# A two-layer decoder trunk on one core: seven block products in the first feed-forward, stacked attention values, state-space tables prepared earlier and read two blocks ahead

## The chip, the core and the metric

The kernel runs on one core of a Trainium2 chip. The core has TensorE (PE in the rows: matrix products, with PEld for its weight loads), VectorE (DVE), ScalarE (ACT), GpSimd (POOL) and the DMA queues, which are fed by SyncE (SP). The metric is the device time of one launch in microseconds (us). Before the change the median of three runs is 2345.22 us (2342.04 to 2348.31).

## The reference

The input is one sequence of 1024 positions with 1024 channels, in float32. There are two layers, each of a mixer and a gated convolutional feed-forward; all add to the residual `x`:

```python
for layer in range(DEPTH):
    i = layer // 2
    if layer % 2 == 0:
        x = x + mla_shortconv_mixer(rms_norm(x, attn_norm[i]), ...)
    else:
        x = x + s5_mixer(rms_norm(x, ssm_norm[i]), ...)
    x = x + conv_ffn(rms_norm(x, ffn_norm[layer]), ...)

def conv_ffn(h, w_up, conv_w, w_down):
    up = causal_depthwise_conv(h @ w_up, conv_w)      # 1024 -> 2 x 2816, width 3
    gate, val = jnp.split(up, 2, axis=-1)
    return (jax.nn.silu(gate) * val) @ w_down
```

The first mixer is causal attention (8 heads, 64 value channels each) beside a short gated convolution. The second is a state-space layer: 64 groups of 16 channels share a complex state of 64. Its coefficients (`exp`, `sin`, `cos` of the inputs `lambda`, `log_step`, and products with `b` and `c`) don't depend on `x`; from them come tables that the layer multiplies with.

## The kernel before

Channels lie on partitions and positions along the rows; the residual stays on the chip as eight tiles `xT0` to `xT7` of 128 x 1024. Each float32 operand of a product is split into a high and a low part (ACT copies the high part, DVE or POOL subtracts), and three of the four part products are summed (`PASSES`). A 128 x 512 product is one `MATMUL`; each has its own weight load.

The stages, in the order of the span: the short convolution with its products (0 to 198 us), attention (to 511.6), the first feed-forward (to 1294), the state-space layer with its gated linear unit (to 1640), the second feed-forward (to the end).

**Short convolution.** `first_units` computes the first three of twelve units (48 matmuls each, line 175) while the norm's sums are still computed; then each of four blocks `m` has three units (`c`, `i`, `b`), which DVE scales (268) and convolves (282 to 290). Two `down` products (190) follow, whose results DVE adds to the residual (193).

**Attention.** Written out by hand under `tc.manual_schedule()`. The values' products (634) take 64 columns of the values' high part or low part as weights, with 128 positions of the probabilities moving, three per block of keys. ACT copies the result (655), splits its high part (657) and POOL its low part (658).

**First feed-forward, `ffn(0, ...)`, 747 on.** The last attention rows go through the output product (`down(last_at, ...)`), with the norm's sums beside it (`Boundary`). Then 44 units of 48 matmuls; DVE scales and convolves each (759 to 764) and multiplies gate and value (808). After each two blocks `down` adds two rows of the second product: eleven groups, 16 evictions each (193). In the gaps `background()` issues one step of `Params` (845 on), which builds the state-space tables: `base` (some 195 small DVE operations on 128 x 32, lines 868 to 891), 16 units (a complex product 1042 to 1047, outer products 1055 to 1060, PE transposes and small products), and 16 `turns` (1055 to 1060 too). The tables go to DRAM.

**State-space layer.** A list `order` fixes the program under `tc.manual_schedule()`. `load_states(m)` and `load_outputs(m)` read the tables of block `m` one block ahead: `et`, `tt` and `co` have one buffer each.

**Second feed-forward.** Class `Pair` (1601 on): gate and value columns of a block and the two halves of positions form a 2 x 2 block product, which takes seven products of 12 matmuls (1648) instead of eight. Sums of weights (1614) and of inputs (`NormBoundary.second_half`, 1504) come first; the gated values go to DRAM (`gfd`) and are read again for the second product in groups of four rows, split again by ACT, DVE and POOL (1794 to 1796).

Outside the sections by hand, a scheduler in the compiler puts each engine's instructions in an order by when they should be ready; each engine then works through its own queue strictly in that order.

## Time and profile before

| | |
|---|---|
| median of the runs | 2345.22 us |
| profiled execution | 2344.66 us, of which the span is 2342.9 |
| PE busy | 2248.5 us (96%) |
| DVE busy | 1614.7 us (69%) |
| ACT, POOL busy | 851.3 us, 767.0 us |
| matmuls on PE | 11228 recorded |

The time of a run is the span of the profile and 1.8 us around it. PE's busy time includes the modelled end of a pipelined matmul, so a stage is read better by its matmuls and by how far apart they start. In the table of stages each engine has its busy time and its instructions in brackets; the granted clock of TensorE is given as a share of 2.4 GHz.

### The profile page before, as it was taken

To read this page: it belongs to the slowest core of one execution; us is meant where nothing else is said; L and a number is where in the kernel's file an instruction comes from. 1 tells how busy PE (TensorE), PEld (TensorE's weight loads), DVE (VectorE), ACT (ScalarE), POOL (GpSimd) and SP (SyncE) were. 2 spreads that over 40 slices of the span, in tenths; PEclk is the share of its full clock that TensorE was granted. 3 is DMA by queue.
4 is the path that set the end of the run, shared out by engine and by line. 5 is a ranking of instruction groups with operands and counts; after the bars stand their busy time and mean duration, and the time that the engine had idled before them with its cause. 6 is when DMAs were issued, how large, how long until landed. Compare 5 with 4: busy or idle time off the path is not lost.

```text
span 2342.9 us, 29810 instructions
## 1 busy us (share of the span) xinstructions
PE 2248.5 (96%) x11228; PEld 1867.9 (80%) x11228; DVE 1614.7 (69%) x2650; ACT 851.3 (36%) x1446; POOL 767.0 (33%) x575
## 2 busy tenths in 40 slices
PE   7999899999999999999999988999789999999999
PEld 6888888888788878888888877788568888878887
DVE  6344677787978778879777487323888888876542
ACT  4112566664232333332223255312444444443110
POOL 4322454435233222232224344431043333324220
PEclk9999999999999999999999998999999999999999
DMA  4112000012122221223332288521132222245301
GB/s 155 45 38 57 1 10 10 10 46 72 29 66 62 82 68 49 76 80 92 101 102 63 93 223 242 171 72 41 54 110 93 82 81 81 81 153 181 125 10 72
DMA packets 227152, 192.04 MB, mean 82 GB/s; under 512 B 25472, under 2 KB 202944, under 8 KB 227008
## 3 DMA queue, kind: packets, MB, share of 16 engines
q1 hardware_dynamic: 227008, 190.14, 26.9%
q8 instruction: 88, 1.44, 0.2%
q14 instruction: 56, 0.46, 0.1%
HBM read 148.22 MB, written 46.07 MB: 83 GB/s over the span
## 4 chain that ended last, share of the span: by engine, by line
PE 79%; DVE 11%; issue 3%; DMA 3%; ACT 3%; POOL 1%; SPq 0%; DVEq 0%; POOLq 0%; ACTq 0%
PE pu L175 31%; PE pd L190 22%; PE pc L1648 4%; PE pb L1648 4%; PE pa L1648 4%; PE pd L1648 2%; PE pu L1554 1%; PE pss L586 1%; PE po L634 1%; PE pckv L378 1%; PE pq L446 1%; PE ptp L615 1%; DVE xT L1696 1%; PE pcq L378 1%; PE pda L644 1%
## 5 line engine op out<-in xcount | busy, mean ns | idle before, releaser
L154 POOL TENSOR_TENSOR wl<-raw,wh 128x1024 fp32r<-128x1024 f32 (+2 forms) x115 | 289.1, 2515 | 487.3 <-ACT wh L153 242.3
L193 DVE TENSOR_TENSOR xT<-pd,xT 128x512 f32<-128x512 f32 x320 | 204.3, 682 | 160.4 <-PE pd L190 159.8
L153 ACT ACTIVATE wh<-raw 128x1024 fp32r<-128x1024 f32 (+2 forms) x117 | 122.4, 1051 | 305.8 <-PE pu L175 212.6
L175 PE MATMUL pu<-f_h,wh 128*128 128x512 f32 x704 | 219.4, 393 | 0.0
L175 PE MATMUL pu<-f_l,wh 128*128 128x512 f32 x704 | 217.2, 390 | 0.0
L175 PE MATMUL pu<-f_h,wl 128*128 128x512 f32 x704 | 216.7, 389 | 0.0
L175 PEld LDWEIGHTS pu<-f_l,wh 128*128 128x128 f32 x704 | 132.1, 188 | 27.9
L175 PEld LDWEIGHTS pu<-f_h,wl 128*128 128x128 f32 x704 | 132.1, 188 | 27.9
L175 PEld LDWEIGHTS pu<-f_h,wh 128*128 128x128 f32 x704 | 130.7, 188 | 28.7 <-issue 1.7
L810 POOL TENSOR_TENSOR gl<-c,gh 128x512 fp32r<-128x512 f32 x44 | 61.4, 1415 | 247.0 <-ACT gh L809 247.0
L1696 DVE SCALAR_TENSOR_TENSOR xT<-u,vec,xT 128x1024 f32<-128x1024 f32 x84 | 111.1, 1330 | 13.3 <-ACT xT L1694 12.6
L759 DVE TENSOR_TENSOR u<-pu,f_rb 128x512 f32<-128x512 f32 x88 | 56.8, 685 | 89.9 <-PE pu L175 87.9
L190 PE MATMUL pd<-gh,wh 128*128 128x512 f32 x352 | 113.5, 403 | 5.4 <-DVE u L759 2.9
L190 PE MATMUL pd<-gh,dwh 128*128 128x512 f32 x352 | 108.8, 390 | 2.5 <-DVE xT L193 1.5
L190 PE MATMUL pd<-gl,wh 128*128 128x512 f32 x352 | 110.4, 395 | 0.0
L190 PE MATMUL pd<-gh,wl 128*128 128x512 f32 x352 | 110.0, 394 | 0.0
L190 PE MATMUL pd<-gh,dwl 128*128 128x512 f32 x352 | 108.5, 389 | 0.0
L190 PE MATMUL pd<-gl,dwh 128*128 128x512 f32 x352 | 108.4, 389 | 0.0
L1796 POOL TENSOR_TENSOR dwl<-raw,dwh 128x1024 fp32r<-128x1024 f32 x20 | 60.8, 3066 | 112.5 <-PE pd L190 84.3
L761 ACT ACTIVATE c<-u,vec 128x512 f32<-128x512 f32 x88 | 59.9, 717 | 69.5 <-DVE u L759 69.1
L190 PEld LDWEIGHTS pd<-gh,wh 128*128 128x128 f32 x352 | 65.8, 191 | 22.6 <-DVE xT L193 4.0
L190 PEld LDWEIGHTS pd<-gh,dwh 128*128 128x128 f32 x352 | 66.1, 188 | 16.9 <-DVE xT L193 1.9
(569 smaller groups left out, 5790.6 us busy)
## 6 DMA issues: line engine op xcount, KB each, us to landing
raw<-in_ffn_w_up_dram SPq DMA_DIRECT2D x50, 512.0 KB, 3.8
raw<-in_ffn_w_down_dram SPq DMA_DIRECT2D x42, 512.0 KB, 4.4
xT<-in_ffn_w_up_dram SPq DMA_DIRECT2D x40, 512.0 KB, 3.6
gfd<-xT SPq DMA_DIRECT2D x21, 512.0 KB, 2.6
raw<-gfd SPq DMA_DIRECT2D x20, 512.0 KB, 4.0
raw<-in_w_glu_dram SPq DMA_DIRECT2D x16, 512.0 KB, 4.0
raw<-in_mix_w_in_dram SPq DMA_DIRECT2D x14, 512.0 KB, 3.9
xT<-in_xt_dram SPq DMA_DIRECT2D x8, 512.0 KB, 7.6
```

Of the source, the lines that this page charges most:

```text
L153: nc.scalar.activation(h[:, 0:n], raw[:, 0:n], AF.Copy)
L154: eng.tensor_tensor(out=l[:, 0:n], in0=raw[:, 0:n], in1=h[:, 0:n].bitcast(F32), op=ALU.subtract)
L175: nc.tensor.matmul(ps[hf], lhsT=w[wi][:, P * k:P * k + P], rhs=xs[k][xi][:, HALVES[hf]], start=(k == 0 and wi == 0 and xi == 0), stop=(k = ...
L190: nc.tensor.matmul(ps[hf], lhsT=ws[i][wi][:, P * f:P * f + P], rhs=gts[i][xi][:, HALVES[hf]], start=(i == first and wi == 0 and xi == 0), ...
L193: nc.vector.tensor_tensor(out=xT[f][:, HALVES[hf]], in0=ps[hf], in1=xT[f][:, HALVES[hf]], op=ALU.add)
L378: nc.tensor.matmul(ps[:, HALF * j:HALF * j + n], lhsT=xa[k][xi][:, P * (2 * p + j):P * (2 * p + j) + P], rhs=w[k // kw][wi][:, n * (k % kw ...
L759: nc.vector.tensor_tensor(out=u[:, 2:HALF + 2], in0=ps[hf], in1=rb[:, HALVES[hf]], op=ALU.mult)
L761: nc.scalar.activation(c, u[:, 2:HALF + 2], AF.Copy, scale=cwcol(layer, 2, m))
L810: nc.gpsimd.tensor_tensor(out=gl[:, cols], in0=cv[hf], in1=gh[:, cols].bitcast(F32), op=ALU.subtract)
L1648: nc.tensor.matmul(ps, lhsT=w[:, HALF * wi + P * k:HALF * wi + P * k + P], rhs=x.at(xi, k), start=(start and k == 0 and wi == 0 and xi == ...
L1696: nc.vector.scalar_tensor_tensor(out=c, in0=u[:, w:S + w], scalar=cwcol(self.layer, w, m), in1=c, op0=ALU.mult, op1=ALU.add)
L1796: eng.tensor_tensor(out=l, in0=raw, in1=h.bitcast(F32), op=ALU.subtract)
```

## The change

Four parts, and in the text that follows they keep their numbers.

1. The first feed-forward uses the code of the second (`FeedForward`, and `Pair` with it): 44 x 42 = 1848 matmuls in the up-product where there were 44 x 48 = 2112. The output product before it is done one half of the positions after the other (16 banks of 512), so that the first half's norm (`sums`, `spread`, `first_half`) can begin before the second is done. The weights of the first blocks are no longer read and split within attention. Gated values go through DRAM, and so does the residual; the second product runs in groups of 2, 4, 4, 4, 4, 2 and 2 rows (112 evictions where there were 176).
2. Values in attention: the high and low parts of the values stand beside each other in one stationary block of 128 columns; two products per block of keys (576 in all) take the place of three (864). The halves of the result are added at the end: ACT copies the lower 64 partitions, DVE adds the upper ones (32 additions of 64 x 256).
3. `Params` in two parts. `base` and units 0 to 7 run in the short convolution: six steps in each of four blocks `m`, the rest in the two `down` products. What they keep goes to DRAM (`kpd`) and comes back. Units 8 to 15 and the turns run in the first feed-forward's second product, one step after each `f`.
4. State-space layer: `et` and `co` get two buffers; the first tables are read during the first units, and then two blocks ahead (`tt` one).

```diff
+        def units(self, first, end):
+            self.end = end
+            self.loaded = self.load(first)
+            for q in range(first, end):
+                yield from self.unit(q)
...
+        def first_part(self):
+
+            yield from self.base()
+            for j in range(2):
+                V.tensor_copy(out=self.apow[j][:, :, 1], in_=self.a[1][j])
+            self.powers(self.apow, ((1, 1, 2, self.a[1]), (1, 2, 3, self.a[2]), (1, 4, 5, self.a[4])))
+            yield
+            yield from self.units(0, SPLIT)
+            nc.sync.dma_start(out=kpd, in_=self.keep)
+            yield
+
+        def second_part(self):
+
+            nc.sync.dma_start(out=self.keep, in_=kpd)
+            yield from self.units(SPLIT, NP // 2)
...
+            yield
+            for q in range(NP // 2):
+                if q % 2 == 0:
+                    j = q // 2
+                    src = kd[:, GC * j:GC * j + P].rearrange("(g c) n -> c g n", c=GC)
+                    nc.sync.dma_start(out=ttd[GC * j:GC * j + GC], in_=src)
+                yield from self.turns(q)
+            yield
+
+    params = Params()
...
+    params.open("a")
+    stages = params.run(params.first_part())
+
+    def background(n=1):
+        for _ in range(n):
+            next(stages, None)
+
...
             ui = scaled(ps_i, "ui")
+            background(2)
...
             held_down = (gts, wr)
         else:
-            down(*held_down)
-            down(gts, wr)
+            down(*held_down, after=lambda f: background(f % 2))
+            down(gts, wr, after=lambda f: background(f % 2))
...
-                    vv = vt.rearrange("p (t i h n) -> p t i h n", t=2, i=4, h=2)
-                    self.vh, self.vl = vv[:, 0], vv[:, 1]
+                    vv = vt.rearrange("p (i h t n) -> p i h t n", t=2, i=4, h=2)
+                    self.vh, self.vl = vv[:, :, :, 0], vv[:, :, :, 1]
+                    self.v = vt.rearrange("p (i h n) -> p i h n", i=4, h=2)
...
             def values(self, po, c0):
                 for kb in range(self.qb + 1):
                     sk = self.steps[kb // 4]
-                    for vi, pi in PASSES:
-                        nc.tensor.matmul(po[0:VD, c0:c0 + P], lhsT=(sk.vh, sk.vl)[vi][:, kb % 4, self.h, :],
+
+                    for pi in range(2):
+                        nc.tensor.matmul(po[:, c0:c0 + P], lhsT=sk.v[:, kb % 4, self.h, :],
                                          rhs=self.pt[kb // 4][pi][:, P * (kb % 4):P * (kb % 4) + P],
-                                         start=(kb == 0 and vi == 0 and pi == 0), stop=(kb == self.qb and vi == 1))
+                                         start=(kb == 0 and pi == 0), stop=(kb == self.qb and pi == 1))
 
...
         def finish_pair(grp, po, hf, i2):
             a32 = small([P, 256], "a32", "a32", 1)
             for h in range(2):
-                nc.scalar.activation(a32[VD * h:VD * h + VD, :], po[0:VD, 256 * h:256 * h + 256], AF.Copy)
+                rows, both = slice(VD * h, VD * h + VD), slice(256 * h, 256 * h + 256)
+                nc.scalar.activation(a32[rows, :], po[VD:P, both], AF.Copy)
...
-            up_first = [split_w(r) for r in up_raw]
...
+    last_rows, last_w = [groups[gr].at for gr in (2, 3)], [w_rows[gr] for gr in (2, 3)]
+    ff = FeedForward(0)
+    for hf in range(2):
+        for f in range(KT):
+            ps = psum("pd")
+            first = 1 if f < 3 else 0
+            for i in range(first, 2):
+                for wi, xi in PASSES:
+                    nc.tensor.matmul(ps, lhsT=last_w[i][wi][:, P * f:P * f + P], rhs=last_rows[i][xi][:, HALVES[hf]],
+                                     start=(i == first and wi == 0 and xi == 0), stop=(i == 1 and wi == 1))
+            if hf and f == 2:
+                ff.sums(0)
+            x = xT[f][:, HALVES[hf]]
+            nc.vector.tensor_tensor(out=x, in0=ps, in1=x, op=ALU.add)
+            ff.add(f, hf)
+            if hf and f == 5:
+                ff.spread(0)
+                ff.first_half()
     if "x1" in dbg:
...
-    down(last_at, w_last, after=bd, skip=3)
...
+    ff.up()
+    groups_d = [(0, 2)] + [(r, r + 4) for r in range(2, 18, 4)] + [(18, 20), (20, 22)]
+    ready_d = ff.begin_down(groups_d[0])
+    params.open("b")
+    stages = params.run(params.second_part())
+    for n in range(len(groups_d) - 1):
+        gts, ws = ready_d
+        last = n == len(groups_d) - 2
+        ready_d = ff.rows(*groups_d[n + 1], ff.d_tile if last else atile)
+        down(gts, ws, after=lambda f: background())
+    for _ in stages:
+        pass
...
-            et, cs = tab("et")[:, 0], tab("cs", 2, 2)
+            et, cs = tab("et", 1, 2)[:, 0], tab("cs", 2, 2)
...
+        def load_tt(m):
+            tables["t", m] = tab("tt")[:, 0]
+            nc.sync.dma_start(out=tables["t", m], in_=ttd[:, 8 * m:8 * m + 8, :])
+
+        def load_co(m):
+            tables["c", m] = tab("co", 1, 2)[:, 0]
+            nc.sync.dma_start(out=tables["c", m], in_=cpd.rearrange("r s g n -> (r s) g n")[:, 8 * m:8 * m + 8, :])
...
-        ps, rb = first_units([split_w(loads.pop(0)()) for m in range(3)], bd.xs, bd, rbp)
+        first_w = [split_w(loads.pop(0)()) for m in range(3)]
+        p5 = p5s.enter_context(phase("ps5"))
+        load_states(0)
+        load_tt(0)
+        load_co(0)
+        raw = [loads.pop(0)()]
+        load_states(1)
+        load_co(1)
+        ps, rb = first_units(first_w, bd.xs, bd, rbp)
...
             states(m)
-            if m + 1 < KT:
-                load_states(m + 1)
+            if m + 2 < KT:
+                load_states(m + 2)
 
         def step_outputs(m):
             emit(m)
             if m + 1 < KT:
-                load_outputs(m + 1)
+                load_tt(m + 1)
+            if m + 2 < KT:
+                load_co(m + 2)
```

The rest of the diff moves `Params`, `Blocks`, the norm's class and `Pair` up in the file and gives them the layer as an argument.

In the order that the compiler gives, the first place is TensorE in the short convolution, block `m` = 1, after its second unit. Before (`a0_h`, `a0_l` are the normed input, `wh`, `wl` the weights):

```order
L175 MATMUL pu_447<-a0_h7_171,wl_444 128x512
L175 MATMUL pu_448<-a0_h7_171,wl_444 128x512
L175 MATMUL pu_511<-a0_h0_124,wh_507 128x512 [waits DVE_49]
L175 MATMUL pu_512<-a0_h0_124,wh_507 128x512 [waits DVE_49]
L175 MATMUL pu_511<-a0_l0_125,wh_507 128x512
L175 MATMUL pu_512<-a0_l0_125,wh_507 128x512
```

And now (`pct`, `pet` and `pk` are the banks of a table's unit; `z0`, `z1` its outer products, `ct` its input):

```order
L175 MATMUL pu_690<-a0_h7_178,wl_687 128x512
L175 MATMUL pu_691<-a0_h7_178,wl_687 128x512
L518 MATMUL pct_788<-ident_72,ct_781 128x64 [waits DMAHW2_49,DMAHW1_49,DVE_49]
L544 MATMUL pet_840<-ident_72,z0_784 128x2x64 [waits DVE_49]
L555 MATMUL pk_849<-z0_784,bd0_804 32x128 [waits DVE_49,Activation_49]
L175 MATMUL pu_861<-a0_h0_131,wh_857 128x512
...
L175 MATMUL pu_861<-a0_l2_144,wh_857 128x512
L544 MATMUL pet_840<-ident_72,z1_785 128x2x64 [waits DVE_49]
L544 MATMUL pet_840<-ident_72,z0_784 128x2x64
L544 MATMUL pet_840<-ident_72,z1_785 128x2x64
```

The third unit of the block now stands behind a transpose and two small products of table unit 0, which wait for DVE.

VectorE in the same stretch; before, from the first block's scaling on (`uc`, `ui`, `ub` are the scaled units, `ut` and `cv` the convolution's):

```order
L268 TENSOR_TENSOR uc_359<-pu_178,a0_rb_324 128x512 [waits Activation_49]
L268 TENSOR_TENSOR uc_359<-pu_179,a0_rb_324 128x512 [waits Activation_49]
L268 TENSOR_TENSOR ui_362<-pu_180,a0_rb_324 128x512
L268 TENSOR_TENSOR ui_362<-pu_181,a0_rb_324 128x512
L282 TENSOR_TENSOR ut_365<-uc_359,ui_362 128x1024 [waits DVE_49]
L285 SCALAR_TENSOR_TENSOR cv_368<-ut_365,vec_84,cv_368 128x1024 [waits Activation_49,Pool_49]
L268 TENSOR_TENSOR ub_372<-pu_298,a0_rb_324 128x512 [waits PE_49]
L287 SCALAR_TENSOR_TENSOR cv_368<-ut_365,vec_84,cv_368 128x1024 [waits DVE_49]
```

And now, the stretch in which `z0` is finished (`keepa` holds the coefficients, `scr` scratch, `om0` a part of the outer product):

```order
L689 TENSOR_TENSOR ut_810<-uc_683,ui_740 128x1024
L304 TENSOR_TENSOR keepa_366<-keepa_366,scr_380 128x32 [waits DVE_49]
L304 TENSOR_TENSOR keepa_366<-keepa_366,scr_380 128x32
L490 TENSOR_TENSOR om1_825<-sr0_786,keepa_366 128x256
L304 TENSOR_TENSOR scr_380<-keepa_366 128x32 [waits DVE_49]
L304 TENSOR_TENSOR scr_380<-keepa_366 128x32
L317 SCALAR_TENSOR_TENSOR keepa_366<-keepa_366 128x32
L491 TENSOR_TENSOR z0_784<-z0_784,om0_824 128x2x128
L304 TENSOR_TENSOR keepa_366<-scr_380 128x32 [waits DVE_49]
L304 TENSOR_TENSOR scr_380<-keepa_366 128x32 [waits DVE_49]
L692 SCALAR_TENSOR_TENSOR cv_813<-ut_810,vec_84,cv_813 128x1024 [waits Activation_49]
L304 TENSOR_TENSOR scr_380<-keepa_366 128x32 [waits DVE_49]
```

Small steps of `base` (128 x 32) and outer products stand between the convolution's operations, each of which waited only for its own input before.

TensorE in attention, a retired item's values; before:

```order
L634 MATMUL po_2220<-ph_2234,vt_1709 64x128 [waits Activation_49]
L634 MATMUL po_2220<-pl_2235,vt_1709 64x128
L634 MATMUL po_2220<-ph_2234,vt_1709 64x128 x2
L634 MATMUL po_2220<-pl_2235,vt_1709 64x128
L634 MATMUL po_2220<-ph_2234,vt_1709 64x128
...
L634 MATMUL po_2220<-pair_2275,vt_1709 64x128 [waits Activation_49]
L634 MATMUL po_2220<-pair_2275,vt_1709 64x128 x5
```

And now, at the same place:

```order
L1048 MATMUL po_3084<-ph_3097,vt_2573 128x128 [waits Activation_49]
L1048 MATMUL po_3084<-pl_3098,vt_2573 128x128
L1048 MATMUL po_3084<-ph_3097,vt_2573 128x128
L1048 MATMUL po_3084<-pl_3098,vt_2573 128x128
...
L1048 MATMUL po_3084<-pair_3137,vt_2573 128x128 [waits Activation_49]
L1048 MATMUL po_3084<-pair_3137,vt_2573 128x128 x3
```

Six and six products with 64 columns of weights (an `x` and a number count equal rows) have become four and four with 128: the output has 128 partitions of `po` now and had 64.

TensorE at the entry of the first feed-forward, which did not exist in this form (`pd` the output product, `f0_st1` the second half's sums, `b11` the first input block, `w1` the split weights of a block):

```order
L1518 MATMUL pd_6528<-ath3_5808,wh_6088 128x512
L1518 MATMUL pd_6528<-atl3_5809,wh_6088 128x512
L1518 MATMUL pd_6528<-ath3_5808,wl_6089 128x512
L1225 MATMUL f0_st1_6609<-ones_77,f0_sq1_6317 128x2 [waits DVE_49]
L1225 MATMUL f0_st1_6609<-ones_77,f0_sq1_6317 128x2 x2
L1451 MATMUL pa_6570<-b11h0_6322,w1_6548 128x512 [waits Activation_49]
L1451 MATMUL pa_6570<-b11l0_6324,w1_6548 128x512
L1451 MATMUL pa_6570<-b11h0_6322,w1_6548 128x512 [waits DVE_49]
L1451 MATMUL pa_6570<-b11h0_6322,w1_6548 128x512
L1451 MATMUL pa_6570<-b11l0_6324,w1_6548 128x512
```

The first block product stands behind the output product and the sums, and waits for ACT's and DVE's splits of input and weights.

## Rows read from the trace of the kernel before

**Rows 1.** Page, part 1: busy us, share of the span, instructions.
```profile
PE 2248.5 (96%) x11228; PEld 1867.9 (80%) x11228; DVE 1614.7 (69%) x2650; ACT 851.3 (36%) x1446; POOL 767.0 (33%) x575
```

**Rows 2.** Stages: length, then each engine's busy us (instructions), clock, DMA share, GB/s.
```profile
1760.00:2095.00 335.00, 333.85 (x1473) 276.11 (x1473) 281.29 (x294) 149.45 (x204) 104.52 (x100) 1.00 0.27 90
```

**Rows 3.** PE's waits, 1640 to 1770 us: total us, times, longest.
```profile
PE pa L1648 <- ACT w L1637: 4.0, 1, 4.0
```

**Rows 4.** Stages, entry of the second feed-forward.
```profile
1640.00:1661.00 21.00, 15.72 (x63) 12.18 (x63) 11.93 (x24) 8.45 (x15) 1.47 (x3) 0.92 0.22 62
1661.00:1760.00 99.00, 83.92 (x324) 62.45 (x323) 89.76 (x122) 46.60 (x70) 27.97 (x20) 0.95 0.28 88
```

**Rows 5.** Stages, entry and body of the first feed-forward.
```profile
623.00:651.00 28.00, 22.84 (x85) 17.43 (x83) 27.69 (x118) 4.65 (x10) 2.99 (x2) 0.88 0.08 20
651.00:1249.00 598.00, 597.74 (x2718) 484.28 (x2717) 470.65 (x897) 181.51 (x367) 182.43 (x89) 1.00 0.28 78
```

**Rows 6.** Groups of DVE, 511.6 to 1294 us: busy, mean ns, idle before.
```profile
L1055 DVE TENSOR_TENSOR z<-sr,ap 128x256 f32<-128x256 f32 (+1 forms) x32 | 18.8, 588 | 0.0
...
L1057 DVE TENSOR_TENSOR z<-sr,ap 128x256 f32<-128x256 f32 (+1 forms) x32 | 15.8, 494 | 1.2 <-DMA cpd<-z 1.1
...
L1045 DVE TENSOR_TENSOR cm<-bt,zi 128x32 f32<-128x32 f32 x16 | 9.6, 597 | 27.0 <-DMA bt<-in_b_re_dram 27.0
...
L1047 DVE TENSOR_TENSOR sr<-cm,cm 128x32 f32<-128x32 f32 x16 | 2.9, 180 | 0.0
```

**Rows 7.** DVE of line 868 alone, 511.6 to 1294 us: length, busy (instructions).
```profile
511.60:1294.00 782.40, 21.56 (x105) 1.00 0.26 71
```

**Rows 8.** Groups of DVE, second feed-forward's second product.
```profile
L193 DVE TENSOR_TENSOR xT<-pd,xT 128x512 f32<-128x512 f32 x95 | 60.8, 684 | 117.2 <-PE pd L190 117.2
L1796 DVE TENSOR_TENSOR gl<-raw,gh 128x1024 fp32r<-128x1024 f32 x20 | 49.7, 2514 | 6.6 <-ACT gh L1795 6.6
```

**Rows 9.** Stages, short convolution after its first units.
```profile
52.80:152.80 100.00, 100.00 (x443) 82.78 (x442) 41.09 (x34) 17.64 (x17) 30.82 (x15) 1.00 0.17 48
152.80:198.00 45.20, 44.95 (x193) 35.79 (x191) 24.02 (x34) 4.77 (x5) 10.24 (x5) 1.00 0.12 33
```

**Rows 10.** PE's timeline, scores in attention: start us, length.
```profile
455.20 0.27 PE L586 MATMUL pss<-kh,qh 96*128 96x128 f32 x1
...
455.54 0.28 PE L590 MATMUL pss<-tri,eye 128*128 128x128 f32 x1
```

**Rows 11.** PE's timeline, values in attention.
```profile
459.22 0.28 PE L634 MATMUL po<-ph,vt 128*64 128x128 f32 x2
459.34 0.22 PE L634 MATMUL po<-pl,vt 128*64 128x128 f32 x1
459.40 0.28 PE L634 MATMUL po<-ph,vt 128*64 128x128 f32 x2
```

**Rows 12.** Groups of PE's weight loads in attention, shapes apart: busy, mean ns.
```profile
L634 PEld LDWEIGHTS po<-pair,vt 128*64 128x64 f32 x432 | 30.2, 135 | 0.4
...
L586 PEld LDWEIGHTS pss<-kl,qh 96*128 96x128 f32 x96 | 18.5, 193 | 1.4
```

**Rows 13.** Stages, attention from 260 us.
```profile
260.00:511.60 251.60, 231.59 (x2007) 211.12 (x2004) 195.90 (x390) 156.39 (x376) 105.26 (x178) 0.99 0.05 16
```

**Rows 14.** Stages, state-space layer to 1500 us.
```profile
1294.00:1400.00 106.00, 100.18 (x510) 84.16 (x509) 61.29 (x91) 41.60 (x53) 45.67 (x25) 0.97 0.58 160
1400.00:1500.00 100.00, 81.35 (x439) 69.90 (x438) 62.90 (x93) 51.95 (x69) 38.66 (x23) 0.90 0.77 223
```

**Rows 15.** PE's waits, 1294 to 1500 us.
```profile
PE px L1288 <- DMA gd<-gy: 9.4, 1, 9.4
```

More of the change, by code (lines that the diff above doesn't have):

```diff
@@ L1708, in hybrid_trunk_kernel @@
-    pairs = [Pair(1, m) for m in range(FIRST + 1)]
-    early = pairs[0:FIRST]
-    for p in pairs:
-        p.weights("12")
-    pps.close()
-    pbk = pps.enter_context(tc.tile_pool(name="psu", bufs=1, space=PSUM, reuse_waits="tile"))
-    def bank_tile(bank, name):
-        return pbk.tile([P, HALF], F32, tag=f"ps{bank}", bufs={"a": 3, "b": 2, "c": 2, "d": 1}[bank], name=name)
-    xb = {"1": nb.b11, "2": nb.b21}
-    for p in pairs:
-        p.product("1", "a", True)
-    nb.sums(1)
-    pbt.close()
@@ L1723, in hybrid_trunk_kernel @@
-    puc = ctx.enter_context(ExitStack())
-    pU = puc.enter_context(phase("pu"))
-    for p in pairs:
-        p.keep()
-    for p in early:
-        p.sums()
-        p.weights("56")
-    blocks = nb.second_half()
-    pairs[0].product("2", "a", False)
-    nb.spread(1)
-    xb["5"] = next(blocks)
-    for p in pairs[1:]:
-        p.product("2", "a", False)
-    xb["6"] = next(blocks)
-    for p in early:
-        p.weights("74")
-    pairs[0].evict()
-    for j in "56":
-        for p in early:
-            p.run(j)
@@ L1743, in hybrid_trunk_kernel @@
-    for p in early:
-        p.weights("3")
-    for j in "74":
-        xb[j] = next(blocks)
-        early[0].run(j)
-        early[1].product(j, "b" if j == "7" else "d", j == "4")
-        if j == "7":
-            early[1].add(early[1].p1, "b", early[1].p1)
-    pairs[FIRST].load(False)
-    pairs[FIRST].sums()
-    pairs[FIRST].weights("65743")
-    xb["3"] = next(blocks)
-    early[0].run("3")
-    early[0].finish()
-    for j in "65":
-        pairs[FIRST].run(j)
-    early[1].evict()
-    early[1].lower("c", HALF)
```

1346 lines of the change are left out of this document (650 added, 696 removed).

## Prediction

> **What bounds the kernel now.** I read the page's busy shares first, then the table of stages, then in each stage that the change touches the waits or groups that price it. The busy shares name the engine: PE is busy for 96% of the span, DVE for 69% [rows 1]. So a removed matmul is a gain of its own length wherever PE runs without a break, and a new wait of PE is a loss of its own length. One stage gives the price of a matmul: from 1760 to 2095 us PE has no gap to speak of and starts 1473 matmuls in 335 us, 0.2274 us each [rows 2]. DVE's mean share hides where it is short: at the entry of the second feed-forward it is busy for 89.8 of 99 us while PE gets only 324 matmuls, 73.7 us' worth [rows 4]; in the short convolution it is busy for 41.1 of 100 and 24.0 of 45.2 us [rows 9]; in the first feed-forward for 470.7 of 598, with PE never short [rows 5]. The change takes matmuls from PE and moves DVE's work about. So the question is where DVE's work lands, and whether PE's queue stands behind it.
>
> **1, the up-product.** 2112 − 1848 = 264 matmuls less, at 0.2274 us: −60.0 us, all on the path, since PE had no gap from 651 us on [rows 5].
>
> **1, the entry.** The same code's entry is to be seen in the second feed-forward: from 1640 to 1760 us it took 120 us for 63 + 324 = 387 matmuls, 88.0 us' worth, so 32 us were lost to waits and to the lower clock behind them (0.92 and 0.95) [rows 4]; the first product waited 4.0 us for a split weight [rows 3]. In the first feed-forward there is less to hide behind. The output product is 78 matmuls, 17.7 us. The first half's sums come after 48 of them, at some 11 us. Then DVE has eight norm multiplications, eight splits and six weight splits of 128 x 512, three evictions and the small chain of the norm. I price the 25 large ones like an eviction of that size, 0.68 us [rows 8], 17 us, and the chain at 3: it ends some 31 us after the start, against 17.7 when PE is done. That is 13 us of waiting where the second feed-forward had 4.0, so 9 more, and I take 12 with the clock that falls in a break of that length. The old entry goes: 5.2 us of gap and 0.12 of 28 us of clock [rows 5], with a little before it some 10 us. Net 32 + 12 − 10 = **+34 us**. Bounds: +15, if the splits hide behind PE as in the second feed-forward and the whole queue is shorter by the weights that are ready; +50, if the second half's norm is late by as much again.
>
> **1 and 3, the second product.** Eviction count falls from 176 to 112; this is DVE's time, not PE's. But DVE gets the splits of the gated values that come back, 2.51 us each [rows 8], and the steps of `Params`. One unit costs DVE (102.9 + 30.8)/16 = 8.4 us: six groups of outer products between 18.8 and 15.8 us, 102.9 together, and six of the complex product between 9.6 and 2.9, 30.8 together [rows 6]. The first group of two rows is 96 matmuls, 21.8 us of PE, and carries eight steps (2.7 units, 22 us), 16 evictions (11 us) and four splits (10 us): 43 us of DVE. The next two groups, 43.7 us of PE each, carry the same 43. So DVE has 129 us of work in 109 us. Evictions lag by the banks that there are, and the ends of DVE's operations overlap by some tenth in the sums of groups, which leaves 116. I take **+8 us**, near what is left of 116 − 109; bounds 0 (the surplus runs off in the lighter groups behind) and +25. A table unit's small products on PE move from one full stage of PE to another: nothing.
>
> **3, the short convolution.** PE had no gap from 52.8 to 198 us, and DVE had 41.1 + 24.0 = 65.1 us of work in these 145.2 us [rows 9]. Added: `base`, some 195 operations at 21.56/105 = 0.205 us [rows 7], 40 us, and eight units at 8.4 us, 67 us. Total 172 us, or 160 with the overlapped ends taken off the added part. Even packed without a gap it is 15 to 27 us more than the stage has. And it isn't packed, since PE stands in line with it. In the new order PE meets the first table unit's three instructions behind block 1's second unit, which at PE's price is near 77 us. They wait for `z0`, behind which stand nearly all of `base` and the convolution's own DVE work of block 0, in one queue that begins near 54 us: 30 us of `base`, 7 us of convolution, some 3 of outer products. So `z0` is ready near 92 to 94 us: 14 us of waiting, and some 5 for the rest of the unit that PE meets within the next twelve matmuls. In blocks 2 and 3 two table units stand ahead of the `b` unit's 48 matmuls in the same way, and DVE, which has 16.8 us of table work and 7 of convolution per block, ends later than PE by some 8 us each. 14 + 5 + 8 + 8 = 35, and a little in the `down` products: **+36 us**. Bounds: +12, the surplus alone with overlaps; +55, if the small operations run as slowly as their worst.
>
> **2, values.** 864 products of 64 weight columns become 576 of 128. Today's pace is in the timeline: three of them from 459.22 to 459.40 us, 60 ns each [rows 11], so 51.8 us. For 128 weight columns and 128 moving ones the nearest row is the scores': three from 455.20 to 455.54, 113 ns each, and I take 110 [rows 10], so 63.4 us. The moving side is the same in both, so the step follows the weights: their load takes 135 ns for 64 columns and 193 for 128 [rows 12]. **+11 us**, since PE is busy for 231.6 of 251.6 us there [rows 13]. The extra ACT and DVE steps at the end of a pair are hidden by DVE's 22% of free time [rows 13]. Bounds: 576 x 60 ns would be −17; +20 if the pairs' new chain ACT, DVE, ACT holds up the bank.
>
> The Trainium skill, TensorE: Matmul & The Clock Gate, section Back-to-back issue gap, states some 81 ns for a matmul of 128 columns in a stream with weight loads; 576 of these would be 46.7 us, so −5 where I have +11, and the sum below 16 us lower. The rows show 113 for the full width, so here the measurement decides.
>
> **4, tables read earlier.** From 1294 to 1500 us PE is busy for 181.5 of 206 us at clocks of 0.97 and 0.90 [rows 14]. The largest wait, 9.4 us, is that of `px`, which reads `et` and the turned inputs, put down to a DMA [rows 15]; the rest are ACT's and DVE's. I take **−8 us**; bounds 0 (the wait was for the turned inputs, which the change doesn't touch) and −20 (all gaps but the splits').
>
> **The sum.** −60 + 34 + 8 + 36 + 11 − 8 = +21 us on the profiled execution's 2344.66: **2366 us**. That execution is 0.6 us under the median of the runs, which I leave out.
>
> **Rivals.** *DVE's steps stay hidden in the short convolution* (faster). The order is the compiler's, which placed PE's waits where it thought the steps ready. If they are, the 36 us are 0 and the time is 2366 − 36 = 2330. For it: PE's 145 us and DVE's 65 leave 80 us of DVE free [rows 9]. Against it: 95 to 107 us are put there. It decides at some 8 us of waiting of PE between 52.8 and 198 us; under that the whole is faster. Chance 0.24, shared with an entry that costs no more than 15.
>
> *Moving columns set the values' pace* (2366 − 28 = 2338). For it: the weight load is drawn beside the matmul before. Against it: the score's 113 ns at the same 128 moving columns [rows 10, 11]. The Trainium skill, in the section named above, gives some 56 ns for an isolated step of 128 columns, which is this rival's pace; the rows of the full width do not show it. Chance 0.08.
>
> *DVE overloaded in the second product* (slower still): the table steps stand ahead of evictions, and PE waits for banks: 25 in place of 8 and the entry at its upper bound, 2366 + 17 to + 33, say 2387. Chance 0.16.
>
> *The tables don't come earlier*, since SyncE's queue holds their reads behind stores: 2374. Chance 0.07.
>
> **Numbers.** The forecast as it stands has 0.43, with its own range 2350 to 2384. About 0.3% (7 us) is what can be told from no change. Slower holds most of the forecast (0.38), the overloaded product and the late tables: 0.61. The same, 2338 to 2352, gets the forecast's lower edge and half of the values' rival and of a partly hidden convolution: 0.14. Faster 0.25. The range has to reach to the hidden convolution and to the overloaded product: 2320 to 2393.
>
> **What would show it.** Up-product between its entry and its end: 44 blocks' halves at 0.227 us a matmul, some 60 us shorter. PE's waits by DVE's `z` at the table's transposes between 75 and 198 us, 30 us or more in all, and the clock under 1.0 there. The values' steps at 110 ns. At the entry of the first feed-forward a wait of 10 us or more ahead of the first block product, and over 40 us lost up to its second block. Evictions waited for in the first groups of the second product. In the state-space layer no 9.4 us wait of `px`. I am wrong if PE has no gap in the short convolution, or if the entry loses no more than the second one does.

## Result and the profile after

The change makes the kernel slower: 2447.99 us median of four runs against 2345.87, a ratio of 1.0437 (95% interval 1.0419 to 1.0455). I had forecast slower, at 2366; the loss is 102 us where I had 21, and the time lies outside the range that I gave, 2320 to 2393. The page of the changed kernel, part 1 (busy us, share of the span, instructions), against [rows 1]:

```profile
span 2445.8 us, 29183 instructions
PE 2242.7 (92%) x10676; PEld 1858.3 (76%) x10676; DVE 1723.4 (70%) x2692; ACT 917.1 (37%) x1538; POOL 721.7 (30%) x612
```

PE has 552 matmuls less on record and is busy for hardly less, over a span that is 103 us longer. The table gives the stages' lengths from the starts of matmuls in the two profiled executions: the convolution to the first product of attention's query compression, attention from there to its last product of values, the feed-forward to the first product of the state-space layer, this to its last output product. Within the feed-forward the second product is counted, in every run alike, from the last `pd` group of the block products on. From there to their end are 24 matmuls, so the count begins 5.4 us before its own first matmul; read from there the up-product took 448.4 us and the second product 290.9.

| stage | before | after | difference | forecast |
|---|---|---|---|---|
| short convolution | 225.9 | 288.4 | +62.5 | +36 |
| attention | 285.5 | 318.1 | +32.6 | +11 |
| first feed-forward | 781.8 | 778.7 (39.5 entry, 442.9 up, 296.3 second product) | −3.1 | −18 |
| state-space layer | 185.8 | 193.1 | +7.3 | −8 |
| gated unit, second feed-forward | 859.1 | 862.7 | +3.6 | 0 |

The stages of the changed kernel, with the columns of [rows 2] (length, busy us of PE, PEld, DVE, ACT and POOL with instructions, granted clock, DMA share, GB/s): convolution, attention, the entry in three pieces, the up-product, the second product in two.

```profile
52.80:258.00 205.20, 167.11 (x746) 131.87 (x745) 146.18 (x432) 42.88 (x113) 39.08 (x20) 0.90 0.22 58
258.00:608.00 350.00, 318.93 (x2195) 295.18 (x2193) 235.14 (x536) 182.00 (x448) 121.06 (x203) 0.94 0.05 14
608.00:646.00 38.00, 23.18 (x94) 18.08 (x94) 29.65 (x46) 16.73 (x28) 15.13 (x12) 0.85 0.50 167
646.00:700.00 54.00, 47.79 (x174) 35.15 (x175) 47.32 (x82) 24.29 (x42) 2.40 (x4) 0.88 0.21 60
700.00:760.00 60.00, 52.10 (x207) 41.39 (x206) 52.81 (x58) 28.44 (x40) 26.83 (x20) 0.91 0.36 113
760.00:1095.00 335.00, 334.82 (x1477) 276.68 (x1475) 281.30 (x293) 150.19 (x205) 104.36 (x100) 1.00 0.27 90
1095.00:1250.00 155.00, 132.04 (x619) 104.67 (x620) 122.97 (x222) 54.48 (x123) 46.54 (x16) 0.93 0.51 157
1250.00:1385.30 135.30, 124.95 (x542) 102.39 (x541) 96.81 (x212) 18.43 (x18) 22.66 (x9) 0.96 0.42 108
```

Two readings. The up-product has taken over the twin's pace to the matmul: 1477 in 335 us, against 1473 in [rows 2]. And the convolution, which ran at a clock of 1.00 with PE never short [rows 9], now has 0.90 and 38 us without a matmul. Who is waited for, in the convolution, in attention, at the entry, in the second product and in the state-space layer (total us, times, longest):

```profile
PE pet L544 <- DVE z L491: 25.3, 3, 15.5
PE pk L555 <- DVE z L491: 10.7, 3, 3.8
PE pk L555 <- DVE z L492: 2.1, 1, 2.1
...
PE po L1048 <- DVE a L1071: 10.4, 14, 1.2
...
PE f_st L1225 <- DVE f_sq L1217: 12.1, 2, 11.6
...
PE pct L518 <- DMA ct<-in_c_im_dram: 20.4, 1, 20.4
...
PE pd L190 <- ACT gh L1367: 10.3, 1, 10.3
...
PE py L1651 <- DMA tt<-ttd: 9.7, 3, 8.4
PE px L1613 <- DMA ut<-ud: 8.8, 1, 8.8
```

The first three are the table units' waits for `z` that were forecast, 38.1 us in all, and the entry's wait was forecast too. The fourth (attention's bank for the values), the sixth and seventh (a DMA and a split in the second product) and the eighth (`tt`) were not. The last, of `px` for the turned inputs `ut`, is the wait that part 4 was to remove.

### The profile page after: what moved, and what is told of

The parts are those of the page before. It is cut to its first block, busy times and chain, and to the rows that moved or that the text cites. A ratio compares the mean times of both kernels' runs of the same rounds, so it can differ in the third digit from the quotient of the medians.

```text
span 2445.8 us, 29183 instructions
## 1 busy us (share of the span) xinstructions
PE 2242.7 (92%) x10676; PEld 1858.3 (76%) x10676; DVE 1723.4 (70%) x2692; ACT 917.1 (37%) x1538; POOL 721.7 (30%) x612
## 4 chain that ended last, share of the span: by engine, by line
PE 72%; DVE 16%; ACT 3%; DMA 3%; issue 3%; POOL 1%; SPq 0%; DVEq 0%; ACTq 0%; POOLq 0%
PE pd L190 19%; PE pu L175 10%; PE pc L1451 9%; PE pb L1451 9%; PE pa L1451 8%; PE pd L1451 4%; PE po L1048 2%; DVE w L1441 1%; PE pu L1777 1%; PE pss L999 1%; DVE xT L1498 1%; PE pda L1058 1%; PE pckv L790 1%; PE pq L858 1%; PE ptp L1028 1%
## 5 line engine op out<-in xcount | busy, mean ns | idle before, releaser
L190 PE MATMUL pd<-gh,dwh 128*128 128x512 f32 x704 | 221.5, 395 | 15.3 <-ACT gh L1367 10.3
L154 POOL TENSOR_TENSOR wl<-raw,wh 128x1024 fp32r<-128x1024 f32 (+2 forms) x49 | 119.5, 2439 | 295.1 <-ACT wh L153 194.2
L190 PEld LDWEIGHTS pd<-gh,dwl 128*128 128x128 f32 x704 | 132.6, 189 | 28.8 <-POOL dwl L1368 1.0
L190 PEld LDWEIGHTS pd<-gl,dwh 128*128 128x128 f32 x704 | 132.6, 189 | 28.6 <-DVE gl L1368 1.0
L1441 DVE TENSOR_TENSOR w<-xT,w 128x512 fp32r<-128x512 f32 x116 | 137.2, 1183 | 0.0
L1451 PE MATMUL pc<-b22h,w 128*128 128x512 f32 x352 | 120.5, 403 | 10.6 <-DVE u L1456 7.2
L1451 PE MATMUL pb<-t3h,w 128*128 128x512 f32 x352 | 119.8, 403 | 7.7 <-ACT t3h L1168 6.6
L1451 PE MATMUL pa<-b11h,w 128*128 128x512 f32 x352 | 119.4, 402 | 4.5 <-ACT w L1440 4.3
L1451 PE MATMUL pb<-t2h,w 128*128 128x512 f32 x352 | 118.3, 396 | 0.8 <-ACT w L1440 0.5
L1451 PE MATMUL pd<-t4h,w 128*128 128x512 f32 x352 | 117.2, 393 | 1.1 <-ACT t4h L1168 1.1
L1451 PE MATMUL pc<-t1h,w 128*128 128x512 f32 x352 | 116.1, 391 | 0.5 <-ACT t1h L1168 0.4
```

Of the source, the lines that this page charges most:

```text
L154: eng.tensor_tensor(out=l[:, 0:n], in0=raw[:, 0:n], in1=h[:, 0:n].bitcast(F32), op=ALU.subtract)
L190: nc.tensor.matmul(ps[hf], lhsT=ws[i][wi][:, P * f:P * f + P], rhs=gts[i][xi][:, HALVES[hf]], start=(i == first and wi == 0 and xi == 0), ...
L1441: nc.vector.tensor_tensor(out=t[:, HALF:S], in0=self.src[j], in1=t[:, 0:HALF].bitcast(F32), op=ALU.subtract)
L1451: nc.tensor.matmul(ps, lhsT=w[:, HALF * wi + P * k:HALF * wi + P * k + P], rhs=x.at(xi, k), start=(start and k == 0 and wi == 0 and xi == ...
```

## The experiments

Each run is one profiled execution unless an interval is given; stages are read as in the table above. The kernel before took between 2337.2 and 2349.4 us on the chips of these single runs, so the stages are compared, and the wholes only roughly.

**Attention: which part of the stacking costs.** First the whole of part 2 undone:

```diff
-                    for pi in range(2):
-                        nc.tensor.matmul(po[:, c0:c0 + P], lhsT=sk.v[:, kb % 4, self.h, :],
+                    for vi, pi in PASSES:
+                        nc.tensor.matmul(po[0:VD, c0:c0 + P], lhsT=(sk.vh, sk.vl)[vi][:, kb % 4, self.h, :],
...
-                nc.scalar.activation(a32[rows, :], po[VD:P, both], AF.Copy)
-                nc.vector.tensor_tensor(out=a32[rows, :], in0=po[0:VD, both], in1=a32[rows, :], op=ALU.add)
+                nc.scalar.activation(a32[VD * h:VD * h + VD, :], po[0:VD, 256 * h:256 * h + 256], AF.Copy)
```

> The changed kernel with part 2 undone: three products of 64 weight columns per block of keys, and the old end of a pair (ACT's copy alone). Attention took 313 us before and 350 with the change. Theory A (the stacking and its longer end are all of it): attention comes back to 312 to 317 us, the whole to 2408 to 2416 us, the granted clock in attention to 0.98 or more. Theory B (the up-weights that are no longer read there, or the late start after the short convolution, have a share): attention stays over 325 us.

Measured: attention 285.8 us (before: 285.5), the entry 34.8 in place of 39.5, the whole 2408.25. Theory A holds: part 2 is all of attention's loss, and 4.7 us of the entry's, whose output product waits for the last pair. Then the stacked products with only the end undone (the second hunk above alone):

> The changed kernel with the stacked products but the old end of a pair: ACT copies the upper half of the bank and nothing is added (this leaves out the low part of the values). It parts the pace of the products from the chain ACT, DVE, ACT behind them. Theory A1 (pace: 576 x 0.112 against 864 x 0.060): attention keeps +12 to +14 us, 326 to 328 us, and no wait of the values' products for DVE. Theory A2 (the 128 columns themselves starve PE and pull the clock down): attention stays over 338 us and the clock under 0.96 although the chain is gone.

Measured: attention 288.7 us, the entry 34.7, the whole 2412.91. Both sizes that I gave are wrong. Without the chain the stage is 2.9 us longer than unstacked, not 12 to 14; with it 32.3. The stage from its first product to its last in the unstacked run, in the stacked one with the old end, and in the changed kernel:

```profile
289.20:575.00 285.80, 264.60 (x2281) 244.27 (x2279) 215.49 (x459) 172.21 (x425) 113.89 (x190) 0.99 0.03 9
290.70:579.40 288.70, 272.53 (x1993) 253.71 (x1991) 213.62 (x459) 172.73 (x425) 111.94 (x190) 0.99 0.03 8
288.40:606.50 318.10, 289.66 (x1992) 266.73 (x1991) 224.30 (x488) 174.76 (x425) 112.69 (x190) 0.94 0.02 8
```

The clock is 0.99 in the first two and 0.94 in the changed kernel. So the chain ACT, DVE, ACT, DVE at the end of a pair costs 29.4 us here and 4.8 at the entry. Its own waits are 10.4 us (the row of `po` for `a` above). In the whole stage PE stands without a product for 28.4 us with the chain and for 16.2 without it, 12 us more; the other 17 us are products that run slower. This second part is not fixed by the chain. Two runs further below have the same code in attention, and with the waits for `a` all but the same (11.2 and 10.4 us) they took 311.0 and 321.4 us there (the base alone in the convolution; no steps in the first group):

```profile
226.30:537.30 311.00, 282.11 (x1992) 259.99 (x1991) 222.33 (x488) 174.77 (x425) 113.06 (x190) 0.97 0.03 8
288.50:609.90 321.40, 292.74 (x1993) 269.60 (x1991) 224.80 (x488) 175.06 (x425) 112.57 (x190) 0.93 0.02 8
```

Against the same 288.7 that is a cost of 22 to 33 us; what decides how far the clock falls no run shows.

The pace of the products was priced right and still did not matter much, as the changed kernel's timeline shows (start, length; consecutive products of values):

```profile
469.87 0.27 PE L1048 MATMUL po<-ph,vt 128*128 128x128 f32 x1
469.98 0.28 PE L1048 MATMUL po<-pl,vt 128*128 128x128 f32 x1
470.09 0.27 PE L1048 MATMUL po<-ph,vt 128*128 128x128 f32 x1
470.20 0.28 PE L1048 MATMUL po<-pl,vt 128*128 128x128 f32 x1
```

They start 110 ns apart, against 60 for the narrow ones [rows 11], just what I took. That is 11.6 us more of PE, of which the stage shows 2.9: the rest filled gaps in which PE waited for others.

**Short convolution: DVE's amount of work, or PE's place in line.** One table unit there and fifteen in the feed-forward:

```diff
-    SPLIT = 8
+    SPLIT = 1
```

> The changed kernel with one table unit (and the base) in the short convolution and the other fifteen in the first feed-forward's second product. Theory A (DVE has more work in the short convolution than the stage is long, seven units are 59 us of it): the short convolution ends at 212 to 222 us in place of 258, and PE waits there only for the first unit, 15 to 20 us. Theory B (PE's queue position, not DVE's amount of work, makes the wait; one unit is enough): it ends over 235 us. In both the feed-forward's second product grows by 40 to 80 us, so the whole is 2430 to 2480 us.

Measured: the convolution's end stands 24.3 us later than before the change (62.5 with eight units); the whole 2457.01, since the tables come late and the state-space layer takes 243 us. In the expectation's count, up to attention's first product, the end is at 222.4 us, and PE waits for the one unit for 19.3 us. These are Theory A's numbers (0.4 us over its range), and Theory B lost by its own; but what the two were about was not decided, since one unit alone costs 24 us. So the base alone (`SPLIT = 0`):

> The changed kernel with the base alone in the short convolution and all sixteen table units in the first feed-forward's second product. With one unit there the convolution's end stood 24 us later than before the change, with eight units 62 us. Theory A (PE's place in line: what costs is that PE meets a table unit before DVE has finished the base; the base by itself is hidden): the end stands 3 to 8 us later than before. Theory B (the base's 40 us of DVE hold up the convolution's own operations): 15 us or more later.

Measured: 226.3 against 225.9, **0.4 us**. That is below even Theory A's range. The base puts 40 us of work on DVE and costs nothing:

```profile
52.80:198.00 145.20, 145.20 (x643) 119.70 (x642) 94.97 (x280) 23.20 (x25) 40.30 (x20) 1.00 0.17 49
```

DVE is busy for 95 of 145 us and PE has no gap. What costs in the change is that PE meets the first unit's instructions before the base is done. The whole was 2447.84, the second product 309.8 and the state-space layer 249.2: sixteen units are too many for the second product. DVE is still at work on the turns when the state-space layer begins, and PE waits there for 51.6 us for the squares of its norm.

**Second product: SyncE's queue, or DVE's load.** The turns' stores on ACT's DMA queue, and the second part's first step issued earlier:

```diff
-                        nc.sync.dma_start(out=dst, in_=wt[j][64 * g:64 * g + 64])
+                        nc.scalar.dma_start(out=dst, in_=wt[j][64 * g:64 * g + 64])
...
     stages = params.run(params.second_part())
+    background()
```

> The changed kernel with two edits for SyncE's queue in the first feed-forward's second product: the turns' stores go through ACT's DMA queue, and the first step of the second part is issued ahead of the first product, so that the table unit's input is read before the next rows. Theory A (waits of 20.4 us for the unit's input and 10.3 us for the last rows are the queue's order): both go, the second product takes 255 to 262 us in place of 290, the whole 2412 to 2422 us. Theory B (DVE's load is the limit, as the prediction had it): other waits take their place and it stays over 278 us.

Measured: 294.3 us in place of 296.3; 2441.82 in all. The wait for the last rows is gone, but the one for the unit's input grew from 20.4 to 25.8 us: the scheduler left its read where it was and moved PE's product ahead. So the second mend did not do what it was made for, and of Theory A only the half on the stores is shown. SyncE's own issues in the changed kernel show the order (start, length):

```profile
1109.83 0.32 SPq L1378 DMA_DIRECT2D raw<-gfd  x1
1110.92 0.33 SPq L1375 DMA_DIRECT2D raw<-in_ffn_w_down_dram  x1
1111.30 0.43 SPq L624 DMA_DIRECT2D keepb<-kpd  x1
1111.78 0.44 SPq L505 DMA_DIRECT2D bt<-in_b_re_dram  x1
1112.26 0.48 SPq L505 DMA_DIRECT2D bt<-in_b_im_dram  x1
1112.78 0.71 SPq L508 DMA_DIRECT2D ct<-in_c_re_dram  x1
1113.53 0.60 SPq L508 DMA_DIRECT2D ct<-in_c_im_dram  x1
```

The reads of the unit's input (`ct`) stand behind the rows' reads, each of which waits for a buffer; PE stood at `pct` since 1098.6 us. So I moved PE's side instead: no steps in the first group.

```diff
-        down(gts, ws, after=lambda f: background())
+        down(gts, ws, after=lambda f: background() if n else None)
```

> The changed kernel with the turns' stores on ACT's DMA queue, and no table steps in the first group of two rows of the first feed-forward's second product (they begin with the second group, and what is left runs at the end). In the run with the other mend the wait for the table unit's input stayed (25.8 us), because its read stood behind the rows' reads as before while PE met the unit as early as before. Theory A (PE's place in line again: a unit that PE meets 96 matmuls later finds its input there): the wait goes, and the second product takes 255 to 265 us in place of 296. Theory B (DVE's load): it takes over 280 us, with waits for evictions or table products in place of it.

Measured (with the stores on ACT's queue): 269.6 us, 26.7 less, and neither wait. Theory A holds, though 4.6 us above its range. The state-space layer lost 6.9 us, all of it ahead of its norm's sums (29.0 us from its first product in place of 21.8); why, no run shows. 2427.94 in all.

**State-space layer: does reading two blocks ahead pay.** Part 4 undone:

```diff
-            if m + 2 < KT:
-                load_states(m + 2)
+            if m + 1 < KT:
+                load_states(m + 1)
```

(and so for `co`, with one buffer for `et` and `co`, and the first reads where they were).

> The changed kernel with part 4 undone: et and co with one buffer, first tables read behind the first units, then one block ahead. From the entry of the state-space layer to its last output product it took 185.8 us before and 193.1 with the change. Theory A (part 4 itself costs the 8.4 us wait for tt, since the reads two ahead stand in SyncE's queue ahead of it): 184 to 187 us, and no wait for tt over 1 us. Theory B (the late stores of part 3 or the entry make it): 190 us or more.

Measured: 185.5 us and no wait for `tt`; 2437.04 in all. Theory A holds: part 4 cost 7.6 us and gave nothing. Then only the rotations one ahead (`load_cs(m + 1)` ahead of `load_states(m + 2)`, which keeps `et`):

> The changed kernel with the rotations' table cs (two buffers) read one block ahead again, and et and co still two ahead. In the changed kernel the read of cs two ahead waits in SyncE's queue for DVE and GpSimd to let go of the buffer, and the read of tt stands behind it. Theory A (this one blocked read delays all behind it): the wait for tt goes and the stage takes 180 to 186 us. Theory B (the reads of tt are late since tt has one buffer): the 8.4 us wait stays and the stage takes 191 to 194 us.

Measured: 187.6 us, 2439.32 in all. The profile names no wait for `tt` any more, but there still is one: the 6.5 us wait of `py` that it puts down to DVE's `g_l` ends as the read of `tt` lands. The first row is from the changed kernel's SyncE queue (the reads of `cs` and the releases of their buffer that they wait for), the others are from this run (issue, its time to landing, product):

```profile
SPq L1587 <- DVE sp L1638: 5.1, 2, 3.0
...
1519.82 0.52 SPq L1600 DMA_DIRECT2D tt<-ttd  x1
...
tt<-ttd SPq DMA_DIRECT2D x1, 512.0 KB, 4.9
...
1524.86 0.76 PE L1655 MATMUL py<-ut,tt 128*128 128x128 f32 x2 [6.52 <-DVE g_l L1676]
```

Issued at 1519.82 us and landed 4.9 us later, the table is there at 1524.7. So Theory A's size holds nearly (1.6 us over its range, and far from B's), its statement on the wait does not: 8.4 us became 6.5, and the wait of `px` fell from 8.8 to 4.3. This read of `tt` goes out 133.3 us after the stage's first product, where it was 140.5 in the changed kernel and 131.3 with part 4 undone. The read of `cs`, which waits in SyncE's queue for its buffer, is therefore most of what held up `tt` behind it, not all. Reading `et` and `co` two ahead still gains nothing over one ahead.

**A version from these findings.** Parts 2 and 4 undone, part 1 kept, and the table's work put where it stands in nobody's line: in the convolution one step where there were two, so that units come late (`SPLIT = 4`); no steps in the first group; the turns mixed in among the units (powers in two halves), their stores on ACT's queue.

```diff
-            background(2)
+            background(1)
...
-    SPLIT = 8
+    SPLIT = 4
```

> Parts 2 and 4 undone, and the tables spread anew: in the short convolution one step where there were two (the base, then four units late, SPLIT = 4); in the second product no steps in the first group, then twelve units with the turns between them on DVE, the turns' stores on ACT's DMA queue, powers in two halves. Theory (PE's place in line: base hidden as in the run with the base alone, 0.4 us; a unit costs little when PE meets it late): the short convolution ends 6 to 20 us later than before (four units are 6 us of PE alone), attention 286 us, the entry 35, the second product 265 to 290, the state-space layer 186 to 200; the whole 2325 to 2365 us. Rival (a unit costs 7.75 us wherever it stands, as eight did 62): the convolution ends 30 us later and the second product takes over 300, the whole 2370 or more.

Measured: 2348.65 beside 2337.2 for the kernel before on that chip, within the range for the whole and yet no gain. The convolution's end is 7.0 us later than before the change, with four units whose products take PE some 5 us: late units cost little beyond their products. The second product took 294.5, 4.5 over its range. With the turns on GpSimd (`outer(..., eng=G)`):

> As the run with the tables spread anew, but the turns' products on GpSimd in place of DVE. Theory (DVE is what is short in the second product; GpSimd has two thirds of its time free there): the second product is 5 to 15 us shorter than with the turns on DVE. Rival (GpSimd needs some 1 us for each of 96 operations, the last turns are late and the state-space layer waits for them, or its operations stretch DVE's): no gain in the second product, and 10 us or more lost at the entry of the state-space layer.

Measured: 305.3 us for the second product, 2357.32 in all. The theory falls: PE's waits for `z` grew from 13.5 to 19.1 us in the sum of its rows, with the state-space layer unchanged (191.3); of the rival the first half holds. Why the waits grew no run shows. Then the turns back on DVE and all spread evenly, with five and six units in the convolution:

> As the run with the tables spread anew, with five units in the short convolution (one step after every f of its second product's second half) and eleven in the feed-forward's second product, units and turns mixed evenly over the forty places that it has. In the earlier run DVE was busy for 91% from the second product's start to 200 us and for 75% behind it, and the product took 294.5 us. Theory (DVE's load where it is bunched): it takes 270 to 284 us, the convolution's end moves by 1 to 6 us, the whole 2325 to 2342 us, 0.2 to 0.9% faster than before the change on the same chip. Rival (each table unit on PE costs by its waits for DVE wherever it stands): 290 us or more and no gain on before.

> As the run with five units in the short convolution, with six there and ten in the second product. DVE's own work in the stretch of the convolution (65 us), the base (40) and six units (6 x 7.3 to 8.4) make 149 to 155 us where the stretch has 145 and six units' PE time of 9. Theory (DVE's sum decides): the convolution's end moves by 6 to 14 us against four units there, the second product takes 4 to 8 us less than with five: no gain on it, within 5 us. Rival (DVE is not full there): the convolution's end moves by 3 us, PE's part of two units, and the whole is 4 us or more faster than with five.

Measured: with five **2324.62** (ratio to before 0.9906, interval 0.9891 to 0.9921), with six 2326.13 (0.9912, 0.9896 to 0.9929). Both are faster than the kernel before by just under 1%, and faster than the changed one. The second product takes 277.2 and 271.6 us, the convolution's end is 8.3 and 13.7 us later than before: with six, what one stage gains the other loses. The expected figures hold (the whole with five units is 0.4 us under its range), but DVE's sum is only a part of the reason: with six units PE waits for 2.5 us in the convolution, and their products take it some 9. Of the 17.3 us that the second product gained with five units against 294.5, some 6 go with the one unit fewer, as the next one shows (5.6). The stages of the version with five, convolution and second product in two pieces:

```profile
52.80:198.00 145.20, 145.20 (x664) 117.30 (x663) 118.50 (x369) 33.30 (x76) 38.88 (x19) 1.00 0.25 66
...
975.00:1100.00 125.00, 116.38 (x511) 92.91 (x509) 112.36 (x210) 43.29 (x68) 34.58 (x16) 0.97 0.56 184
1100.00:1260.00 160.00, 159.90 (x750) 127.87 (x749) 137.71 (x332) 41.09 (x113) 27.27 (x10) 1.00 0.42 110
```

In the convolution DVE is busy for 118.5 of 145 us, over four fifths, and PE still has no gap and a clock of 1.00; the changed kernel's 205 us hold 146 of DVE's and lost 38 of PE's.

## Why the prediction was wrong

The sign came out, but four terms of the sum were too small: the convolution (+36, measured +62.5), the values (+11, measured +32.6 in attention), the second product (+8, measured some 33) and the tables (−8, measured +7.3). In the first the wait was priced rightly and what comes with it was left out; in the other three the wait that came was not in the term at all. By the prediction's own steps, in their order:

- *What bounds the kernel*: right for the most part. PE, with DVE behind it: in the convolution, in attention and at the entry PE waits for DVE. In the second product and the state-space layer it waits for DMA reads, which this step did not have.
- *Up-product, −60*: right. The pace was the expected one and the stage without a gap.
- *Entry, +34*: right in size. From 608 to 760 us 94 + 174 + 207 = 475 matmuls, 108 us' worth, took 152: 44 lost, and 32 + 12 had been forecast. 4.7 of it came from attention's longer end. The wait itself stood elsewhere: 11.6 us at the second half's sums, not at the first block product behind them. So the size came out in part by luck.
- *Second product, +8*: **wrong**. With entry and up-product at 482.4 us (in the table's count), the forecast of the whole feed-forward (781.8 − 18) leaves 281 us for it; it took 296.3. And some 11 us of table products, which I had left in it, had moved to the convolution, so the term was about 25 too low, and some 33 in place of 8 would have been right. I priced DVE's load. What cost was order: PE met the table unit 12 matmuls into the product, and its input stood in SyncE's queue behind reads that wait for buffers (20.4 us, and a lower clock after it); the last rows' reads stood behind the turns' stores (10.3). The run without steps in the first group, with the turns' stores on ACT's queue, took 26.7 us of it away with the same work on DVE, bar its place (6.9 of them came back in the state-space layer). I had a rival on SyncE's queue for part 4 and none here.
- *Convolution, +36*: right in its waits (38.1 us: 15.5 and 3.8 at the first unit, 9.0 and 7.6 in blocks 2 and 3, 2.1 in the `down`), wrong in the sum: +62.5. Some 11 are the units' products on PE, which I had counted as nothing, since the feed-forward has as many less. The remaining 13 are, all but 2, products at the lower clock behind the waits, which I had priced at the entry only. In the trace 44 of the stage's block products take over 0.3 us to the next one, 7 us more than at 0.227, and the units' products take 15 us in place of 11. And the reason that I gave as the floor, DVE's sum against the length of the stage, did not set this length: DVE was busy for 146 of 205 us. Whether it would bind for eight units that PE meets late no run shows; four of them and the base cost 7.0 us, five 8.3, six 13.7.
- *Values, +11*: the term was the pace, and it held (110 ns); its effect was 2.9 us. The sentence that failed is that the extra ACT and DVE steps "are hidden by DVE's 22% of free time". This chain was not hidden by free time of its engines: it holds the bank, PE waits 14 times for at most 1.2 us, and the clock falls. It cost 29.4 us (22 and 33 in two other runs), nearly three times the term it was left out beside. The upper bound, +20, had this chain as its reason and was too low: attention lost 32.6.
- *Tables, −8*: **wrong** sign, +7.3. The wait of `px` that was to go was for the turned inputs, as its lower bound said; in the changed kernel it is still there. The new wait is in the rival that reads stand behind others in SyncE's queue, but not behind stores: for the most part behind a read two blocks ahead that waits for its own buffer.

So the sign of the whole rested on the convolution and the entry, whose waits were right. Measured minus forecast by stage: convolution +26.5 (13, nearly all of clock, 11 of table products, the rest waits), attention +21.6, first feed-forward +15 (25 of the second product, less the 11 that had left it), state-space layer +15.3, and the 3.6 behind it, which no run took apart: 82 us in all. The rivals: none of them was the one that came; the overloaded second product gave the nearest time, by another mechanism.

## What to carry to other kernels

Work that is moved under another stage is paid by where its instructions stand in the queues of the engines that wait, more than by the busy share of the engine that does it: the base's 40 us of DVE cost 0.4, one unit met too early 24, four met late 7. With six met late PE had waits again, if only 2.5 us, so DVE's sum is still to be worked out as a limit. Before loads are brought forward, look what each waits for in its own queue: here a read that had to wait for a buffer delayed the reads behind it. And every new wait of PE is to be priced with the slow products behind it.

## What had not been expected of the hardware

After the long waits of this trace PE's products start at about half the pace for a while. Behind the 15.5 us wait of the changed kernel's convolution (start, length, pairs of products):

```profile
98.47 1.22 PE L175 MATMUL pu<-a_h,wh 128*128 128x512 f32 x2
99.49 1.06 PE L175 MATMUL pu<-a_l,wh 128*128 128x512 f32 x2
100.34 1.06 PE L175 MATMUL pu<-a_h,wl 128*128 128x512 f32 x2
101.20 1.06 PE L175 MATMUL pu<-a_h,wh 128*128 128x512 f32 x2
102.05 0.76 PE L175 MATMUL pu<-a_l,wh 128*128 128x512 f32 x2
102.65 0.63 PE L175 MATMUL pu<-a_h,wl 128*128 128x512 f32 x2
103.12 0.62 PE L175 MATMUL pu<-a_h,wh 128*128 128x512 f32 x2
```

Pairs are 0.85 us apart and then 0.46, so four pairs cost some 1.6 us more; this is the lower of the clock's two levels, 1.2 GHz (the granted clock is 0.50 from 98 to 102 us), and then the higher. That it falls was known from the kernel before; that it also falls in attention, where no wait for a bank was longer than 1.2 us (0.94 in the mean against 0.99 without the chain, and 0.97 and 0.93 in two runs with the same code there), was not expected.
